# One layer of a hybrid decoder trunk: TensorE held to the program's order in the attention loop, with the value products of an earlier step placed between the score tiles

## The chip, the cores and the metric

The kernel runs on one core of a Trainium2 chip. The metric is the device time of one execution in microseconds (us); the kernel before has a median of 2955.1 us over three runs (2953.64 to 2956.42). Five engines work beside each other on that core: TensorE (PE, with its weight loads as PEld), VectorE (DVE), ScalarE (ACT), GpSimd (POOL) and SyncE (SP), which here issues most DMAs.

## The reference, cut to what matters

One layer, SEQ = 2048, D_MODEL = 1024. What the change touches is the FoX attention of eight heads of width 64 (causal, a learned decay as a bias of the logits, swept in 128-query blocks):

```python
def block(args):
    qi, ci, i = args
    s = jnp.einsum('bhqd,bhkd->bhqk', qi, kh).astype(jnp.float32) * scale
    s = s + ci[..., :, None] - c[:, :, None, :]
    qpos = i * Q_BLOCK + jnp.arange(Q_BLOCK)
    s = jnp.where(kpos[None, :] <= qpos[:, None], s, -jnp.inf)
    pr = jax.nn.softmax(s, axis=-1).astype(vh.dtype)
    return jnp.einsum('bhqk,bhkd->bhqd', pr, vh)
...
x = x + mix @ w_out[i]
x = x + jnp.square(jax.nn.relu(hm @ w_up[i])) @ w_down[i]
x = x + sigmoid(rmsnorm(x, g_ple[i]) @ w_ple_gate[i]) * (p[i] @ w_ple[i])
```

Before the attention come the input projections and an mLSTM of four heads; behind it come the output projection, the MLP and the gate.

## The kernel before, in words

The program is written with a tile framework. It is recorded engine by engine in the order of the Python code; a scheduler then chooses the order in which each engine's instructions stand, by its own estimate of when their operands are ready, and inserts semaphores. At run time each engine takes its instructions strictly in that fixed order.

The attention (the stage from 560 to 1323 us) works on pairs of heads: `for j in range(NP)` calls `fox_attn` (line 882), which goes over two heads and, within a head, over nine steps, the entries of `ROWS` (line 779). A step is one or two blocks of 128 queries whose key blocks add up to 16: query block 15 alone, then 14 and 0, 13 and 1, and so on to 8 and 6, and at last 7 alone (8 key blocks).

`fox_rows` (line 781) makes a step's probabilities. A **score tile** is a PSUM tile `s` of up to four key blocks (three buffers, `SB`): two TensorE products (lines 798 and 800, high and low part of the keys), a third for the diagonal (line 803), and one DVE instruction (line 806) that adds the `bias` tile, writes the sum to `sp` (SBUF, four buffers of eight key blocks, `SPB`) and keeps the running row maximum. Most steps have five score tiles, a head has 40. Then come `nb` (DVE, line 818), the exponentials (ACT, line 821), a 16-bit high part (ACT, line 826) and low part (POOL, sometimes DVE, line 828) in `ph` (four buffers), and a transposing DMA on SP's queue to `pt` (line 830, three buffers, eight key blocks each; two a step). A head has 17 of these units.

`fox_av` (line 834) makes the **value products** of a step: for each key block three small TensorE products (lines 846, 847, 849) from `pt`, and a copy to `og` (line 852). They run three steps late (`LAG`): `drain(LAG)` (line 856) is called at the end of each step. With three `pt` buffers, the transpose of a unit waits until the value products of the unit three before it are done.

`fill` (line 958) puts other TensorE work between score rows and value products, spread evenly over a pair's steps: for pairs 0 to 2 the projections of the next pair (`zfq`, `zv`, `zfk`, lines 260 and 271) and the embeddings (`pp`), for the last pair half of the output projection (`om`, line 641).

At the start of a head two `bias` tiles (two buffers) are loaded on SP's queue (line 890) and scaled on DVE (line 893). `bias_1` holds keys 1024 to 2047, `bias_0` keys 0 to 1023. `bias_0` of a new head takes the buffer that the last step (query block 7) of the head before it reads, so it can be loaded only after that step's DVE work, and the new head's first score tile needs it. At the end of a pair `second_keys` (lines 691 and 693) also puts the new keys of the second head in place on DVE.

Of the kernel before, what the change touches and what calls it, by code (L numbers as in the profile page):

```python
# [54 lines left out]
def hybrid_layer(ctx, tc, x, p, w_in, b_fox_f, b_mlstm_i, b_mlstm_f, w_conv, g_mix,  # L55
# [722 lines left out]

    ROWS = ((15,),) + tuple((14 - i, i) for i in range(7)) + ((7,),)

    def fox_rows(fl, fpp, h, rows, bias, fs, qkl):


        Qt, Kt, KL = qkl
        tag = f"{h}_{rows[0]}"
        nu = (sum(rows) + len(rows) + 7) // 8
        st = [fl.tile([P, 1024], F32, tag="sp", name=f"sp{tag}_{u}", bufs=SPB)
              for u in range(nu)]
        at = 0
        for r, i in enumerate(rows):  # L790
            qs = slice(i * P, (i + 1) * P)
            mx, kb, parts = None, 0, []
            while kb <= i:
                u, o = divmod(at + kb, 8)
                n = min(4, 8 - o, 8 - kb % 8, i + 1 - kb)
                ps = fpp.tile([P, 512], F32, tag="s", name=f"s{tag}_{r}_{kb}", bufs=SB)
                ks = slice(kb * P, (kb + n) * P)
                PE.matmul(ps[:, 0:n * P], lhsT=Qt[:, qs], rhs=Kt[:, ks], start=True, stop=False)  # L798
                diag = kb + n > i
                PE.matmul(ps[:, 0:n * P], lhsT=Qt[:, qs], rhs=KL[:, ks], start=False,  # L800
                          stop=not diag)
                if diag:
                    PE.matmul(ps[:, (n - 1) * P:n * P], lhsT=identb, rhs=fneg, start=False,
                              stop=True)
                m = fl.tile([P, 1], F32, tag="mx", name=f"mx{tag}_{r}_{kb}", bufs=8)
                V.tensor_tensor_reduce(out=st[u][:, o * P:(o + n) * P], in0=ps[:, 0:n * P],  # L806
                                       in1=bias[kb // 8][:, kb % 8 * P:(kb % 8 + n) * P],
                                       scale=1.0, scalar=-3.0e38 if mx is None else mx,
                                       op0=ALU.add, op1=ALU.max, accum_out=m)
                mx = m  # L810
                if parts and parts[-1][0] == u:
                    parts[-1][2] = o + n
                else:
                    parts.append([u, o, o + n])
                kb += n
            at += i + 1
            nb = fl.tile([P, 1], F32, tag="nb", name=f"nb{tag}_{r}", bufs=8)
            V.tensor_scalar(nb, mx, fs[:, 1:2], LN_P, op0=ALU.mult, op1=ALU.add)  # L818
            for u, o0, o1 in parts:
                sl_ = st[u][:, o0 * P:o1 * P]  # L820
                A.activation(sl_, sl_, AF.Exp, bias=nb, scale=fs[:, 0:1])  # L821
        pts = []
        for u in range(nu):
            ph = fl.tile([P, 2048], F16, tag="ph", name=f"ph{tag}_{u}", bufs=PHB)
            cnt[0] += 1
            A.copy(ph[:, 0:1024], st[u])  # L826
            eng = V if cnt[0] % DM == 3 else T
            eng.tensor_sub(ph[:, 1024:2048], st[u], ph[:, 0:1024])  # L828
            pt = fl.tile([P, 16, P], F16, tag="pt", name=f"pt{tag}_{u}", bufs=PTB)
            SP.dma_start_transpose(out=pt, in_=ph)  # L830
            pts.append(pt)
        return pts

    def fox_av(fl, fpp, h, rows, pts, vt, ogs):

        if not avt:
            avt.append(fpp.tile([P, 2, 2, P], F32, name="av", bufs=1))
        slot[0] ^= 1
        aps = avt[0][:, slot[0]]
        at = 0  # L840
        for r, i in enumerate(rows):
            ar = aps[:, r, 0:65]
            for kb in range(i + 1):
                pt, o = pts[(at + kb) // 8], (at + kb) % 8
                vs = vt[:, kb, (h % 2), :]
                PE.matmul(ar, lhsT=pt[:, o, :], rhs=vs[:, 0:65], start=kb == 0, stop=False)  # L846
                PE.matmul(ar[:, 1:65], lhsT=pt[:, o, :], rhs=vs[:, 65:129], start=False,
                          stop=False, skip_group_check=True)
                PE.matmul(ar, lhsT=pt[:, 8 + o, :], rhs=vs[:, 0:65], start=False, stop=kb == i)
            at += i + 1  # L850
        for r, i in enumerate(rows):
            V.tensor_copy(ogs[i // 4][:, i % 4, h % 2, :], aps[:, r, 0:65])
# [3 lines left out]
    def drain(n):  # L856
        while sum(e[0] for e in avq) > n or (avq and not avq[0][0]):
            e = avq.pop(0)
            if e[0]:
                fox_av(*e[1:])  # L860
            else:
                posts.append([PD_, *e[1:]])

# [18 lines left out]
    def fox_attn(fl, fpp, j, z, fill):  # L882
        fs, iv, vt, qkls = z
        ogs = {}
        for hh in range(2):
# [7 lines left out]
                V.tensor_scalar(b, b, fs[:, 2:3], None, op0=ALU.mult)  # L893
                bias[sg] = b
            for k, rows in enumerate(ROWS):
                pts = fox_rows(fl, fpp, h, rows, bias, fs, qkls[hh])
                for i in rows:
                    if hh == 0 and i // 4 not in ogs:
                        ogs[i // 4] = fl.tile([P, 4, 2, FD + 1], F32, tag="og",
# [3 lines left out]
                if hh == 1 and k in DONE:  # L903
                    g = DONE[k]
                    avq.append((0, fl, j, g, ogs[g], iv))
                drain(LAG)
                late()
                if h == FH - 2 and k == LK:
                    loads.append(mix_load(0, NP - 1))
# [2 lines left out]
        if j == NP - 1:  # L912
            for _ in loads[0]:
                pass
            for k in range(LAG - 1, -1, -1):
                fill(FE)
                drain(k)
                late()
            fill(1e9)
            late(all_=True)  # L920
# [36 lines left out]
    with phase("fl", 2) as fl, phase("fps", 2, PSUM) as fpp:  # L957
# [13 lines left out]
        for j in range(NP):  # L971
# [6 lines left out]
            else:  # L978
                for _ in mix_load(NP, KT):
                    pass  # L980
                fill = filler(late_parts(), FT)
            fox_attn(fl, fpp, j, box[0], fill)
            fill(1e9)
            second_keys()
            box = nxt
# [207 lines left out]
```

## Time and profile before

| what | before |
|---|---|
| median of 3 runs | 2955.1 us |
| the profiled execution's own time | 2954.44 us |
| its span, first to last instruction | 2952.7 us |
| PE busy | 2698.4 us (91%) |
| DVE busy | 1621.7 us (55%) |
| ACT busy | 1008.3 us (34%) |
| POOL busy | 698.7 us (24%) |
| mean granted TensorE clock | 0.968 of full speed |

The span is the time on the core; the execution's own time lies 1.74 us above it. The profile gives busy time by engine, the idle time before an instruction with what ended it, and for a chosen stretch the same with the granted clock and the DMA engines' busy share. PE's busy time is modelled (matmuls are pipelined), so its idle time is the safer figure.

### The profile page before, as it was taken

The numbers are of one execution on the slowest core, as the hardware profiler recorded it, in microseconds if no ns is written. First come the engines' busy times: TensorE is split into PE (matmuls) and PEld (weight loads), VectorE is DVE, ScalarE is ACT, GpSimd is POOL, SyncE is SP. The second block draws the span as 40 slices with busy tenths as digits, with TensorE's granted clock in tenths as the row PEclk, the third lists the DMA queues.
The fourth block names the chain that finished last, engine by engine and source line by source line (L and its number), as shares of the span: only waits on it lengthen the run. The fifth ranks groups of instructions, "written<-read, shape, count | busy, mean of one in ns | idle before, by whom it ended". The sixth has DMA issues, their size and how long they took to land. (4 is left out here: it accounts for less than half of the span.)

```text
span 2952.7 us, 45034 instructions
## 1 busy us (share of the span) xinstructions
PE 2698.4 (91%) x18229; PEld 1507.1 (51%) x18229; DVE 1621.7 (55%) x3633; ACT 1008.3 (34%) x1686; POOL 698.7 (24%) x435
## 2 busy tenths in 40 slices
PE   4998999888878788788999999999999999999997
PEld 2756767555454554343344444444444444444686
DVE  6464654766757657556654444444444444445636
ACT  6244444465555555553411111111111111113532
POOL 1011110244343444343122111111212111111132
PEclk9999999989899989999999999999999999999999
DMA  9212220387686879996700000000000000002623
GB/s 243 45 44 59 58 47 20 94 167 137 139 166 133 165 169 219 196 205 222 148 29 29 29 29 16 28 15 29 29 29 29 29 29 16 28 15 43 143 69 136
DMA packets 535265, 256.36 MB, mean 87 GB/s; under 512 B 432784, under 2 KB 502672, under 8 KB 535056
## 3 DMA queue, kind: packets, MB, share of 16 engines
q1 hardware_dynamic: 525296, 236.66, 35.0%
q10 hardware_dynamic: 9760, 16.82, 1.8%
q8 instruction: 142, 2.33, 0.3%
q14 instruction: 67, 0.55, 0.1%
HBM read 113.88 MB, written 32.60 MB: 50 GB/s over the span
## 5 line engine op out<-in xcount | busy, mean ns | idle before, releaser
L1054 PE MATMUL d<-wd_hl,hid 128*128 128x512 f16 x3072 | 678.2, 380 | 8.4 <-DVE x L1059 8.2
L1036 PE MATMUL h<-y1t,wu_hl 128*128 128x512 f16 x3072 | 673.5, 379 | 0.5 <-issue 0.5
L1054 PEld LDWEIGHTS <-hid 128*128 128x128 f16 x3072 | 301.3, 98 | 375.0 <-issue 15.8
L1036 PEld LDWEIGHTS <-wu_hl 128*128 128x128 f16 x3072 | 300.5, 98 | 363.2 <-ACT y1y L200 1.0
L1059 DVE SCALAR_TENSOR_TENSOR x<-d,fac,x 128x512 f32<-128x512 f32 x512 | 373.8, 747 | 132.2 <-PE d L1054 131.8
L1044 POOL TENSOR_TENSOR hid<-r,hid 128x512 f16<-128x512 f32 x128 | 174.5, 1364 | 765.2 <-ACT hid L1043 659.1
L1042 DVE SCALAR_TENSOR_TENSOR r<-h,r 128x512 f32<-128x512 f32 x128 | 88.3, 690 | 458.2 <-ACT r L1040 458.1
L1040 ACT ACTIVATE r<-h 128x512 f32<-128x512 f32 x128 | 75.9, 594 | 766.8 <-PE h L1036 763.3
L828 POOL TENSOR_TENSOR ph<-sp,ph 128x1024 f16<-128x1024 f32 x119 | 255.9, 2164 | 283.3 <-ACT ph L826 219.3
L271 PEld LDWEIGHTS <-yt 128*128 128x128 f16 x3072 | 251.6, 101 | 40.1 <-issue 13.7
L260 PE MATMUL zqk<-yt,wqk_hl 128*128 128x512 f16 x768 | 188.7, 393 | 27.9 <-DMA yt<-yy 27.9
L821 ACT ACTIVATE sp<-sp,nb,fs 128x1024 f32<-128x1024 f32 (+3 forms) x192 | 177.9, 982 | 85.2 <-DVE nb L818 60.5
L798 PE MATMUL s<-K,Q 128*128 128x512 f16 (+3 forms) x320 | 117.9, 369 | 79.4 <-DVE mx L806 76.4
L846 PE MATMUL av<-vt,pt 128*128 128x65 f16 x1088 | 121.9, 199 | 67.3 <-DMA pt<-ph 55.6
L271 PE MATMUL zvo<-wvo_hl,yt 128*128 128x256 f16 x1536 | 175.0, 275 | 4.1 <-ACT wvo_hl L155 2.8
L1007 PE MATMUL pg<-wpg_hl,y2t 128*128 128x256 f16 x1536 | 171.0, 275 | 4.7 <-DVE x L1059 4.0
L1007 PEld LDWEIGHTS <-y2t 128*128 128x128 f16 x1536 | 151.6, 99 | 24.1 <-issue 5.1
L826 ACT CAST ph<-sp 128x1024 f16<-128x1024 f32 x136 | 137.8, 1038 | 67.9 <-DMA pt<-ph 62.6
L846 PEld LDWEIGHTS <-pt 128*128 128x128 f16 x1088 | 105.3, 100 | 75.1 <-DMA pt<-ph 67.8
L806 DVE CUSTOM_DVE_ANT_0 sp<-s,bias,mx 128x512 f32<-128x512 f32 (+2 forms) x192 | 124.5, 648 | 29.4 <-POOL ph L828 14.2
L260 PEld LDWEIGHTS <-wqk_hl 128*128 128x128 f16 x768 | 77.4, 101 | 105.5 <-ACT wqk_hl L155 25.9
L641 PEld LDWEIGHTS <-mix 128*128 128x128 f16 x768 | 76.4, 102 | 101.6 <-issue 27.7
(380 smaller groups left out, 3648.2 us busy)
## 6 DMA issues: line engine op xcount, KB each, us to landing
x<-in_x_dram SPq DMA_DIRECT2D x32, 512.0 KB, 5.8
wu_st<-in_w_up_dram SPq DMA_DIRECT2D x16, 1024.0 KB
wd_st<-in_w_down_dram SPq DMA_DIRECT2D x16, 1024.0 KB, 4.9
bias<-crow SPq DMA_DIRECT2D x16, 512.0 KB, 5.9
pled<-fox_st ACTq DMA_DIRECT2D x32, 256.0 KB, 2.8
wod<-spare ACTq DMA_DIRECT2D x32, 256.0 KB, 5.0
wos<-wod SPq DMA_DIRECT2D x32, 256.0 KB, 3.9
emb<-pled SPq DMA_DIRECT2D x32, 256.0 KB, 3.0
```

What stands on the lines that cost most here:

```text
L260: PE.matmul(ps, lhsT=hl[:, a, kt, m * P:(m + 1) * P], rhs=yT[g][b][:, kt, :], start=i == 0, stop=i == 3 * KT - 1)
L271: PE.matmul(ps[:, 0:n], lhsT=yT[g][b][:, kt, o:o + P], rhs=hl[:, a, kt, 0:n], start=i == 0, stop=i == 3 * KT - 1)
L806: V.tensor_tensor_reduce(out=st[u][:, o * P:(o + n) * P], in0=ps[:, 0:n * P], in1=bias[kb // 8][:, kb % 8 * P:(kb % 8 + n) * P], scale=1.0 ...
L821: A.activation(sl_, sl_, AF.Exp, bias=nb, scale=fs[:, 0:1])
L826: A.copy(ph[:, 0:1024], st[u])
L828: eng.tensor_sub(ph[:, 1024:2048], st[u], ph[:, 0:1024])
L846: PE.matmul(ar, lhsT=pt[:, o, :], rhs=vs[:, 0:65], start=kb == 0, stop=False)
L1007: PE.matmul(ps, lhsT=aT[t // 4][ya][:, kt, o:o + P], rhs=hl[:, wa, kt, :], start=i == 0, stop=i == 3 * KT - 1)
L1036: PE.matmul(ps, lhsT=wu[:, a, kt, m * P:(m + 1) * P], rhs=y1T[g][b][:, kt, :], start=i == 0, stop=i == 3 * KT - 1)
L1044: T.tensor_sub(hid[:, 1, m], r2, hid[:, 0, m])
L1054: PE.matmul(ps, lhsT=hid[:, a, m, t * P:(t + 1) * P], rhs=wd[:, b, m, hf * 512:(hf + 1) * 512], start=i == 0, stop=i == 5)
L1059: V.scalar_tensor_tensor(xs, ps, fac, xs, ALU.mult, ALU.add)
```

## The change: what it does

Three edits go together. The attention of a pair is recorded under `manual_schedule` for PE, so that TensorE's instructions keep the order of the Python code there, while the other engines are still ordered by the scheduler. `fox_av` becomes a generator that pauses after five key blocks, then after every further five, counted over the step's 16 (`(at + kb) % 5 == 4`). And `fox_rows` is handed the generator of the step three back and takes one piece from it behind each score tile from the second on; what is left of it is done before `fill`. No instruction of TensorE is added or removed: both programs have 35645 rows on it.

```diff
-    def fox_rows(fl, fpp, h, rows, bias, fs, qkl):
+    def fox_rows(fl, fpp, h, rows, bias, fs, qkl, av):
...
-        at = 0
+        at = chunks = 0
         for r, i in enumerate(rows):
...
                 kb += n
+                chunks += 1
+                if chunks > 1:
+                    next(av, None)
...
                 PE.matmul(ar, lhsT=pt[:, 8 + o, :], rhs=vs[:, 0:65], start=False, stop=kb == i)
+                if (at + kb) % 5 == 4:
+                    yield
...
     def drain(n):
         while sum(e[0] for e in avq) > n or (avq and not avq[0][0]):
             e = avq.pop(0)
             if e[0]:
-                fox_av(*e[1:])
+                yield from fox_av(*e[1:])
...
             for k, rows in enumerate(ROWS):
-                pts = fox_rows(fl, fpp, h, rows, bias, fs, qkls[hh])
+                av = drain(LAG - 1)
+                pts = fox_rows(fl, fpp, h, rows, bias, fs, qkls[hh], av)
+                for _ in av:
+                    pass
...
                     avq.append((0, fl, j, g, ogs[g], iv))
-                drain(LAG)
                 late()
...
-                drain(k)
+                for _ in drain(k):
+                    pass
...
-            fox_attn(fl, fpp, j, box[0], fill)
+            with tc.manual_schedule(engines={mybir.EngineType.PE}):
+                fox_attn(fl, fpp, j, box[0], fill)
```

First place: TensorE in a step in the middle of head 1 (query blocks 12 and 2). `s1_12_0_8` is head 1, step 12, its first query block, key block 8; `pt1_15_0` is the first transposed unit of the step that began with query block 15; `zv1` are projections for the next pair. Only the first product of a run stands here, without weight loads and without rows that repeat. Before:

```order
L798 MATMUL s1_12_0_0_7564<-K_5163,Q0_5162 128x512
L798 MATMUL s1_12_0_4_7569<-K_5163,Q0_5162 128x512
L798 MATMUL s1_12_0_8_7574<-K_5163,Q0_5162 128x512
L798 MATMUL s1_12_0_12_7579<-K_5163,Q0_5162 128x128
L271 MATMUL zv1_14_7610<-fox_hl_5118,yt3_333 128x128
L798 MATMUL s1_12_1_0_7589<-K_5163,Q0_5162 128x384
L271 MATMUL zv1_15_7636<-fox_hl_5118,yt3_333 128x128
L846 MATMUL av_6239<-vt0_5167,pt1_15_0_7087 128x65
L846 MATMUL av_6239<-vt0_5167,pt1_15_1_7092 128x65
```

All 16 key blocks of value products stand behind the step's projections. In the changed program:

```order
L798 MATMUL s1_12_0_0_7566<-K_5163,Q0_5162 128x512
L798 MATMUL s1_12_0_4_7571<-K_5163,Q0_5162 128x512
L849 MATMUL av_6178<-vt0_5167,pt1_15_0_7134 128x65
L798 MATMUL s1_12_0_8_7591<-K_5163,Q0_5162 128x512
L849 MATMUL av_6178<-vt0_5167,pt1_15_1_7139 128x65
L798 MATMUL s1_12_0_12_7611<-K_5163,Q0_5162 128x128
L798 MATMUL s1_12_1_0_7636<-K_5163,Q0_5162 128x384
L271 MATMUL zv1_14_7661<-fox_hl_5118,yt3_333 128x128
L271 MATMUL zv1_15_7687<-fox_hl_5118,yt3_333 128x128
```

The value products now stand in pieces between the score tiles, and the projections come last and whole.

Second place: TensorE where head 1 ends and head 2, of the next pair, begins. Before:

```order
L798 MATMUL s1_7_0_4_8208<-K_5163,Q0_5162 128x512
L846 MATMUL av_6239<-vt0_5167,pt1_10_0_7869 128x65
L798 MATMUL s2_15_0_4_8370<-K_5163,Q1_5944 128x512
L846 MATMUL av_6239<-vt0_5167,pt1_10_1_7874 128x65
L798 MATMUL s2_15_0_8_8375<-K_5163,Q1_5944 128x512
L260 MATMUL zfq2_0_8525<-yt0_135,fox_hl_5118 128x512
L846 MATMUL av_6239<-vt0_5167,pt1_9_0_7993 128x65
L846 MATMUL av_6239<-vt0_5167,pt1_8_0_8117 128x65
...
L798 MATMUL s2_15_0_12_8380<-K_5163,Q1_5944 128x512
```

In the changed program:

```order
L798 MATMUL s1_7_0_4_8210<-K_5163,Q0_5162 128x512
L849 MATMUL av_6178<-vt0_5167,pt1_10_0_7921 128x65
L849 MATMUL av_6178<-vt0_5167,pt1_10_1_7926 128x65
L798 MATMUL s2_15_0_4_8375<-K_5163,Q1_5944 128x512
L849 MATMUL av_6178<-vt0_5167,pt1_9_0_8045 128x65
L798 MATMUL s2_15_0_8_8395<-K_5163,Q1_5944 128x512
L849 MATMUL av_6178<-vt0_5167,pt1_9_1_8050 128x65
L798 MATMUL s2_15_0_12_8415<-K_5163,Q1_5944 128x512
L849 MATMUL av_6178<-vt0_5167,pt1_8_0_8169 128x65
```

Before, projections and the value products of three steps stand between the third and the fourth score tile of the new head; now the fourth tile follows after two blocks of `pt1_9_1`.

Third place: SP's queue at the same boundary. Before:

```order
L830 DMA_TRANSPOSE pt1_8_1_8122<-ph1_8_1_8119 128x16x128
L830 DMA_TRANSPOSE pt1_7_0_8220<-ph1_7_0_8217 128x16x128
L716 DMA fox_st_5119<-in_w_in_dram 128x8x128
L890 DMA bias2_0_8360<-crow_382 128x1024
L945 DMA_TRANSPOSE po0_3_8296<-po0_3_8296 128x8x128
```

In the changed program:

```order
L833 DMA_TRANSPOSE pt1_8_1_8174<-ph1_8_1_8171 128x16x128
L716 DMA fox_st_5119<-in_w_in_dram 128x8x128
L895 DMA bias2_0_8365<-crow_382 128x1024
L953 DMA_TRANSPOSE po0_3_8298<-po0_3_8298 128x8x128
L833 DMA_TRANSPOSE pt1_7_0_8237<-ph1_7_0_8234 128x16x128
```

The load of `bias_0` no longer stands behind the transpose of the last step; it stands behind that of `pt1_8_1`, which waits for the value products of `pt1_9_0`.

In the last pair the `om` products move too: before, eight of them stand ahead of the value products of head 6's first step; now one or two stand behind each step.

## Rows read from the trace of the kernel before

**Rows 1.** Busy time by engine, granted clock, DMA share, GB/s: the whole attention stage.

```profile
559.90:1323.40 763.50, 609.60 (x6333) 370.39 (x6331) 490.96 (x1521) 416.05 (x531) 309.10 (x159) 0.92 0.80 163
```

**Rows 2.** PE's waits in the stage: total us, times, longest.

```profile
PE s L798 <- DVE mx L806: 76.4, 43, 4.9
PE av L846 <- DMA pt<-ph: 55.6, 35, 6.6
PE av L846 <- DVE og L852: 11.6, 6, 3.1
```

**Rows 3.** PE in order of time, one step of head 3: start, us, [idle before].

```profile
897.09 0.38 PE L260 MATMUL zfk<-yt,fox_hl 128*128 128x512 f16 x1
898.93 0.38 PE L798 MATMUL s<-K,Q 128*128 128x512 f16 x1 [1.47 <-DVE mx L806]
...
900.11 4.70 PE L260 MATMUL zfk<-yt,fox_hl 128*128 128x512 f16 x21
904.64 0.19 PE L846 MATMUL av<-vt,pt 128*128 128x65 f16 x1
...
906.12 0.38 PE L798 MATMUL s<-K,Q 128*128 128x512 f16 x1
```

**Rows 4.** Busy times in the seven head boundaries (last tile to next head's fourth): two, and sum.

```profile
733.10:753.50 20.40, 14.94 (x165) 8.67 (x162) 15.95 (x46) 5.04 (x7) 5.68 (x4) 0.92 0.96 176
...
1213.20:1238.50 25.30, 17.01 (x186) 9.31 (x185) 5.88 (x15) 10.13 (x11) 8.16 (x4) 0.87 1.09 227
sum 149.70, PE 100.64 PEld 66.47 DVE 75.87 ACT 49.36 POOL 45.37; mean PE 14.38 PEld 9.50 DVE 10.84 ACT 7.05 POOL 6.48
```

**Rows 5.** DVE in order of time at the boundary of heads 1 and 2.

```profile
733.07 0.07 DVE L806 DVE_READ_ACCUMULATOR2_ANT mx<- 128x1 f32 x1
...
750.96 0.75 DVE L893 TENSOR_SCALAR bias<-bias,fs 128x1024 f32<-128x1024 f32 x1 [1.31 <-DMA bias<-crow]
...
752.71 0.69 DVE L806 CUSTOM_DVE_ANT_0 sp<-s,bias 128x512 f32<-128x512 f32 x1
```

**Rows 6.** PE's wait at the end of that boundary.

```profile
753.47 0.39 PE L798 MATMUL s<-K,Q 128*128 128x512 f16 x1 [3.16 <-DVE mx L806]
```

**Rows 7.** SP's queue in order of time at the boundary of heads 6 and 7.

```profile
1220.50 10.31 SPq L830 DMA_TRANSPOSE pt<-ph  x3
1230.91 0.54 SPq L890 DMA_DIRECT2D bias<-crow  x1
```

**Rows 8.** The lines of the bias load and of the transposes: duration ns min/median/max; landing.

```profile
L890 SPq DMA_DIRECT2D bias<-crow x16: 332/639/1447, 540.8 to 1230.9; - x16
...
DMA to landing us min/median/max: 5.4/5.9/6.6
...
L830 SPq DMA_TRANSPOSE pt<-ph x136: 1317/2472/7229, 584.4 to 1313.0; - x136
...
DMA to landing us min/median/max: 4.3/5.2/10.1
```

**Rows 9.** DVE's groups in the stage: line, operation, count, busy us, mean ns, idle before.

```profile
L806 DVE CUSTOM_DVE_ANT_0 sp<-s,bias,mx 128x512 f32<-128x512 f32 (+2 forms) x192 | 124.5, 648 | 29.4 <-POOL ph L828 14.2 <-PE s L803 3.4 <-PE s L800 1.9
L806 DVE DVE_READ_ACCUMULATOR2_ANT mx<- 128x1 f32 x320 | 26.2, 82 | 0.0
L693 DVE COPY K<-K 64x512 f16<-64x512 f16 x14 | 13.2, 942 | 0.3
L691 DVE SCALAR_TENSOR_TENSOR KL<-zfk,K 64x512 f16<-64x512 f32 x14 | 9.7, 695 | 0.7 <-ACT K L690 0.3
```

**Rows 10.** Busy times in the stage's first 30 us.

```profile
559.90:590.00 30.10, 24.41 (x115) 10.48 (x113) 22.37 (x56) 16.41 (x20) 11.19 (x6) 0.95 0.20 45
```

**Rows 11.** Busy times and granted clock around PE's longest wait of the stage.

```profile
839.00:846.00 7.00, 1.98 (x44) 1.81 (x40) 1.89 (x2) 1.77 (x3) 1.56 (x1) 1.00 1.22 201
846.00:853.00 7.00, 5.43 (x75) 5.43 (x76) 0.85 (x4) 0.28 (x1) 0.00 (x0) 0.51 1.15 204
```

**Rows 12.** PE's waits in two stretches inside heads 6 and 7: total us, times, longest.

```profile
PE av L846 <- DMA pt<-ph: 8.6, 8, 2.0
...
PE av L846 <- DMA pt<-ph: 12.7, 6, 4.4
```

## The prediction

> **What bounds the kernel now.** I read the busy times of the stage first, then TensorE's waits in it, then single steps and the boundaries between heads in order of time. The change moves TensorE's work in the attention alone, a stretch of 763.5 us in which PE is busy 609.6, DVE 491.0, ACT 416.1 and POOL 309.1 [rows 1]. No engine is full: PE, the busiest, is idle for 763.5 - 609.6 = 153.9 us, and what ends its idle time is two things [rows 2]. In 43 waits of 76.4 us together a score tile waits for DVE, which has not yet read one of the three PSUM tiles. In 41 waits of 67.2 us value products wait for a transposed unit, or for the copy of the accumulator before them.
>
> One step shows the first kind [rows 3]. Three score tiles go out, the fourth waits 1.47 us for DVE, then come the projections (21 products in 4.70 us) and only then the value products, whose 16 key blocks take from 904.64 to 906.12, 1.48 us. So 1.48 us of work that doesn't need the score tiles stands behind the wait, in every step.
>
> The second place where PE stands still is between heads. Seven times DVE has no score tile to read until the new `bias_0` is there. These windows last 149.7 us together, with PE busy for 100.6 and so idle for 49.1 [rows 4]. PE is that busy there because the scheduler put projections and the value products of three steps between the new head's third and fourth tile. At the boundary of heads 1 and 2 the last tile of one head ends on DVE at 733.14, the scaling of `bias_0` starts at 750.96, and the first tile of the next head follows at 752.71 [rows 5]; PE's own wait at its end is 3.16 us [rows 6].
>
> **The change, part by part.** No instruction is added, so only waits can change.
>
> *Score tiles inside heads.* Of the 76.4 us of waits for DVE about 18 lie in the boundaries (six waits like that of [rows 6]), which leaves some 58 us in 37 waits, 1.6 us each. In the new order five key blocks, 5 / 16 x 1.48 = 0.46 us, stand ahead of each of the third, fourth and fifth tile: up to 1.4 us of each wait is filled. The waits are uneven (the longest is 4.9), many shorter than 1.4 and some much longer, so I take 1.15 us off each: -43 us. DVE can follow: a score tile costs it 0.65 + 0.08 = 0.73 us [rows 9], while PE's pair of score products and one piece take 0.43 + 0.46. Bounds: -58, if every wait goes; -15, if DVE is late by more than the pieces fill, since its order is still the scheduler's and weight preparation and norms stand between the tiles.
>
> *Boundaries.* Here holding the order costs. The fourth tile of the new head now follows the third after one piece, and everything behind it, projections too, waits with it. What it waits for is a chain: value products of `pt_9_0` done, `pt_8_1` issued on SP (2.5 us, the median), `bias_0` issued and landed (5.9), scaled (0.75), the first tile read (0.73) [rows 8, 5, 9]: 9.9 us, with 0.2 of PE's work beside it. That is four boundaries inside a pair at 9.7 us, 39 us. Between pairs DVE also has up to four pairs of key copies (0.70 + 0.94 each) [rows 9], a norm and a weight reduction ahead of `bias_0`; from the 19.6 us of [rows 5] I take off the transpose that no longer stands ahead of the load, and the waits for copies of value products, and come to about 15 from the last tile to the first. PE reaches its fourth tile some 2 us after that last tile, so it stands still for about 13 us, and 11 where a projection is left: 38 for three. Together 77 against 49: +28. The load itself gets earlier: before, it stood behind three transposes issued in 10.3 us [rows 7]. Bounds: +0 (7 us each), +60 (15.6 each).
>
> *Start of the stage.* In the first three steps there are no value products yet. Before, projections fill them, with 24.4 us busy in the first 30 [rows 10]; in the new order 14 score tiles and two projections, some 17 us of work, stand there. +7 us; bounds 0 and +13.
>
> *Waits for transposed units inside heads.* Value products come a fill (4 to 5 us) earlier against their step's scores, but the `pt` buffers they free come free as much earlier, so a steady step gains and loses alike: a transpose lands 5.2 us after its issue [rows 8], and is wanted a step later. In the last pair the new order helps. There 14 waits cost 21.3 us [rows 12], since eight `om` products had been used up at its start; they are now spread over the steps. I take half: -10. Bounds: -38 (about all such waits in heads), and +25, where SP's queue, with a transpose of 2.5 us twice a step and other loads between, becomes late.
>
> *Clock.* TensorE's granted clock is 0.92 in the stage [rows 1], that is 16% of the time, some 122 us, at 1.2 GHz. It fell after PE had stood still: in the 7 us behind the longest wait (6.6 us [rows 2]) it is 0.51 [rows 11]. Fewer waits inside heads, longer ones between them: -8 us, with bounds -30 and +10. The Trainium skill ("TensorE: Matmul & The Clock Gate", HAM oscillation) says that matmul bursts separated by waits start each time at the low clock, which speaks against the new order: seven longer stops, each followed by slow products. The trace agrees with it at [rows 11], where 5.4 busy us at half clock cost 2.7; by the rule alone, counting only the seven stops, the term would be +19 instead of -8.
>
> Sum: -43 + 28 + 7 - 10 - 8 = -26 us. The profiled execution took 2954.4 us (span 2952.7), 0.7 below the median of the runs shown: 2928 against it, **2929 us** against the median. What lies ahead of the stage keeps its order; behind it nothing but the starting time changes.
>
> **The rivals.** *The likeliest, as above* (0.45): 2929, own range 2908 to 2948.
>
> *More is gained* (0.18). Every stall inside a head feeds the next through three rings of buffers (`sp`, `ph`, `pt`); with value products earlier, units come free before they are wanted. Then score waits go (-58), waits for units inside heads halve (-19), the clock gives 20, boundaries and start cost what I took (+35): -62, 2893. For it: long stretches of rows where a transposed unit is waiting for its reader, not the reverse (41 waits on 136 units). Against it: DVE at 64% of the stage comes in bursts.
>
> *Slower: the boundary* (0.22). If PE stands still for s us at each of seven boundaries, the sum is 7 s - 49 - 43 + 7 - 10 - 8 = 7 s - 103: it turns at s = 14.7. The price of a boundary rests on one SP queue and one DVE order, neither of which is held. If `pt_8_1` comes late (its issue took up to 7.2 us [rows 8]) and key copies stand ahead of `bias_0`, s is 18, and the time is 2955 + 23 = 2978. For it: before, DVE's gaps are 20 to 25 us [rows 4] and PE was kept busy in them by the reordering that is now forbidden. Against it: part of each gap was the wait for transposes and value products that are now earlier.
>
> *No change* (0.15). The scheduler had already filled what there is, and a wait covered in one place comes back at the next, because the step is set by the chain from score tile through DVE, ACT, POOL and the DMA and not by PE's order; or score waits shrink by about 15 and the boundary takes them: within 6 us of 2955. For it: PE is idle only 20% of the stage.
>
> **How the numbers follow.** A measurement of this kernel can tell about 0.2%, 6 us, from no change. Faster by more: 0.45 + 0.18 = 0.63; within: 0.15; slower: 0.22. The bounds of the terms don't all fall on one side together, so the range reaches to the two rivals and a little past the first: 2885 to 2976, which leaves out less than a tenth at each end.
>
> **What would show it.** Right: PE's waits for DVE in the stage fall from 76 us to below 50, boundaries included, with none over 2 us inside heads; each boundary shows one wait of PE of 9 to 13 us ahead of a new head's fourth tile, ended by DVE; DVE's gap from the last tile to the next head's first falls from 19.6 to about 15; the stage, from first score product to last value product, takes about 737 us. The forecast is wrong if the boundary waits exceed 15 us, if waits for `pt` grow by more than 25 us, or if DVE's order, chosen anew, leaves score waits above 1.4 us in most steps.

## The result, and the profile after

| what | before | after |
|---|---|---|
| median | 2954.6 us (4 runs) | 3025.5 us (4 runs, 3020.9 to 3035.8) |
| ratio, 95% interval | | 1.025, 1.0231 to 1.0269 |
| profiled execution's own time | 2954.4 us | 3022.5 us |
| attention, first score product to last value product | 763.5 us [rows 1] | 830.4 us |
| PE idle in it | 153.9 us | 212.2 us |
| DVE busy | 1621.7 us | 1625.7 us |

The changed kernel is 2.5% slower; 66.9 of the 68.1 us by which the profiled executions differ lie in the attention. Its row answers to [rows 1]:

```profile
558.80:1389.20 830.40, 618.16 (x6326) 381.42 (x6325) 492.92 (x1530) 416.25 (x531) 312.15 (x159) 0.85 0.73 151
```

The engines do the same work in a longer time. PE's busy time rose by 8.6 us at a granted clock of 0.85 (0.92 before), its idle time by 58.3. PE's waits in that stretch (total us, times, longest), against [rows 2]:

```profile
PE s L798 <- DVE mx L806: 155.1, 43, 15.8
PE av L849 <- DMA pt<-ph: 25.2, 16, 6.1
PE av L849 <- DVE og L857: 14.0, 9, 4.2
PE pp L609 <- DVE vt L763: 11.5, 3, 6.1
```

Waits for transposed units halved (55.6 to 25.2); waits of a score tile for DVE doubled. They are of two kinds. **At the seven head boundaries** one wait each, 69.1 us together. The busy times in the stretches from a head's last tile to the next head's fourth follow: the counterparts of the two in [rows 4], and the sum of all seven.

```profile
748.20:762.45 14.25, 1.69 (x32) 1.21 (x32) 13.47 (x35) 3.50 (x4) 4.88 (x4) 0.67 0.77 178
...
1268.80:1286.30 17.50, 6.60 (x59) 3.73 (x56) 4.32 (x7) 4.98 (x6) 6.29 (x3) 0.68 1.11 230
sum 105.62, PE 23.46 PEld 14.52 DVE 56.70 ACT 24.41 POOL 25.65; mean PE 3.35 PEld 2.07 DVE 8.10 ACT 3.49 POOL 3.66
```

The stretches are shorter than before (149.7 us), but PE is idle in 105.6 - 23.5 = 82.2 us of them, against 49.1.

**Inside heads**, that is in all other score waits, they grew too, from 58.3 us to 86.2 (gaps below 0.15 us counted, which the listing leaves out). A stop ahead of a step's fifth score tile shows how. DVE in order of time, then PE:

```profile
683.76 0.69 DVE L806 CUSTOM_DVE_ANT_0 sp<-s,bias 128x512 f32<-128x512 f32 x1 [1.12 <-PE s L800]
684.37 0.08 DVE L806 DVE_READ_ACCUMULATOR2_ANT mx<- 128x1 f32 x1
687.39 0.42 DVE L582 TENSOR_REDUCE pm<-plsp 128x1 f32<-128x256 f32 x1 [2.93 <-DMA plsp<-in_p_dram]
687.72 0.74 DVE L806 CUSTOM_DVE_ANT_0 sp<-s,bias,mx 128x512 f32<-128x512 f32 x1
```

```profile
685.05 0.27 PE L798 MATMUL s<-K,Q 128*128 128x256 f16 x1
...
688.53 0.37 PE L798 MATMUL s<-K,Q 128*128 128x256 f16 x1 [3.04 <-DVE mx L806]
...
689.01 2.23 PE L271 MATMUL zv<-fox_hl,yt 128*128 128x128 f16 x19
```

DVE has read the first tile and waits 2.93 us for an embedding's load (`pm`), while three finished tiles fill the three buffers. PE stands ahead of the fifth for 3.04 us, though the projections behind it (`zv`) need nothing of all this. I laid DVE's instructions beside each wait of PE inside heads. Of the 86.2 us DVE read score tiles in 21.9, did other work in 34.5 and stood waiting in 29.8; before, 58.3 us were 21.3, 22.0 and 14.9. So the whole growth of 27.9 us stands beside DVE's other work and DVE's other waits. DVE's own waits in the stage show the reverse side:

```profile
DVE sp L806 <- PE s L800: 70.2, 29, 6.5
DVE bias L898 <- DMA bias<-crow: 46.4, 9, 8.4
DVE fss L939 <- POOL psq L937: 31.6, 9, 7.7
...
DVE pm L582 <- DMA plsp<-in_p_dram: 19.5, 7, 4.5
```

Before, DVE waited 4.6 us for score tiles and 72.8 for value products. Now it waits 70.2 for score tiles: while PE works through a step's projections in one piece, DVE has nothing to read; when the tiles come, it is often at other work, and PE waits. In the trace of before, projections (those for the embeddings and the output counted too) stand at 191 places between two score products, in that of after at 59.

### The profile page after: what moved, and what is told of

Same layout as the page of the kernel before. It is cut to its first block, busy times and chain, and to the rows that moved or that the text cites. A ratio compares the mean times of both kernels' runs of the same rounds, so it can differ in the third digit from the quotient of the medians.

```text
span 3020.8 us, 45085 instructions
## 1 busy us (share of the span) xinstructions
PE 2703.5 (89%) x18229; PEld 1517.1 (50%) x18229; DVE 1625.7 (54%) x3633; ACT 1008.1 (33%) x1686; POOL 701.5 (23%) x435
## 5 line engine op out<-in xcount | busy, mean ns | idle before, releaser
L1063 PE MATMUL d<-wd_hl,hid 128*128 128x512 f16 x3072 | 675.8, 379 | 11.8 <-DVE x L1068 11.5
L849 PE MATMUL av<-vt,pt 128*128 128x65 f16 x1088 | 137.2, 202 | 40.0 <-DMA pt<-ph 25.2
L829 ACT CAST ph<-sp 128x1024 f16<-128x1024 f32 x136 | 136.6, 1037 | 17.8 <-DMA pt<-ph 17.4
L806 DVE CUSTOM_DVE_ANT_0 sp<-s,bias,mx 128x512 f32<-128x512 f32 (+2 forms) x192 | 124.5, 649 | 24.6 <-POOL ph L831 10.0
L850 PE MATMUL av<-vt,pt 128*128 128x64 f16 x1088 | 137.0, 203 | 0.0
L852 PE MATMUL av<-vt,pt 128*128 128x65 f16 x1088 | 136.2, 201 | 0.0
```

The source lines that it names most:

```text
L1063: PE.matmul(ps, lhsT=hid[:, a, m, t * P:(t + 1) * P], rhs=wd[:, b, m, hf * 512:(hf + 1) * 512], start=i == 0, stop=i == 5)
```

## The experiments

Theory: held to a fixed order, PE can't go around a stop of DVE; the loss is DVE's other work ahead of score tiles inside heads, and the chain through `bias_0` at the boundaries. Rivals, numbered in the expectations: the value products between the tiles themselves; the order chosen for DVE; the fixed order as such; the boundaries alone. The medians of the kernel before, run again beside each group of these runs, lay between 2950.7 and 2954.7 us; ratios are against it, with 95% intervals. "Boundary waits" are PE's waits ahead of a new head's fourth score tile, "inside heads" are all its other waits of score tiles for DVE.

### The two halves of the change

```diff
# e1: from the changed kernel
-            with tc.manual_schedule(engines={mybir.EngineType.PE}):
-                fox_attn(fl, fpp, j, box[0], fill)
+            fox_attn(fl, fpp, j, box[0], fill)
# e2: to the kernel before
+            with tc.manual_schedule(engines={mybir.EngineType.PE}):
+                fox_attn(fl, fpp, j, box[0], fill)
```

> The new placement of the value products, but TensorE ordered by the scheduler again. My theory (the loss is the fixed order: TensorE can no longer put projections between score tiles while DVE works on something else): 2945 to 2965 us; TensorE's waits of score tiles for DVE in the attention back from 155 to 70 to 95 us, the seven boundary waits back from 69 to about 20. Rival 1 (the value products between the score tiles are themselves what slows the step): 3000 to 3030, score waits above 130.

Measured: 2966.0 us, ratio 1.0049 (1.0033 to 1.0065).

> TensorE held to the program's order, but the value products at the end of the step as before the change. My theory: the fixed order costs the more the less stands between the score tiles, so this is slower than the changed kernel: 3040 to 3100 us, score waits 180 to 250 us. Rival 1 (the interleaving costs, not the order): 2955 to 2990. Rival 2 (interleaving makes no difference at all): 3015 to 3035.

Measured: 3057.7 us, 1.0361 (1.0343 to 1.0378). PE's waits, e1 (two rows), then e2:

```profile
PE s L798 <- DVE mx L806: 69.1, 52, 5.4
PE av L849 <- DMA pt<-ph: 67.4, 50, 4.1
```

```profile
PE s L798 <- DVE mx L806: 193.4, 83, 18.2
```

The fixed order alone costs 3.6%; the new placement takes 32 us of that back. In e2's trace the waits inside heads are 122.3 us and those at the boundaries 71.8, against 58.3 and 19.5 in the kernel before; with the pieces between the tiles, in the changed kernel, they are 86.2 and 69.1. So the pieces fill 36 us of waits inside heads, and the fixed order had first added 64. With the order free, the placement costs 0.5%, just above the expected span, and it shows as waits for units (55.6 to 67.4), not for DVE. Rival 1 falls: the hold is what costs.

### What stops TensorE inside heads

e5 takes much of DVE's other work out of the attention: maxima and scales become constants, the norm goes, and differences go to POOL, so that its output is no longer that of the layer. The core of the edit, called lean below:

```diff
-        pw, sc = pow2_scale(mp, npart, name)
+        if leanf[0]:
+            pw, sc = one[:, 0:1], one[:, 3:4] if name.startswith("wo") else one[:, 1:2]
...
-        V.tensor_sub(hl[:, 1], sf, hl[:, 0])
+        (T if leanf[0] else V).tensor_sub(hl[:, 1], sf, hl[:, 0])
...
-            V.tensor_reduce(pm, pin, axis=AX.X, op=ALU.max, apply_absolute_value=True)
...
+            psc, pe = one[:, 2:3], pec
...
-            eng = V if cnt[0] % DM == 3 else T
+            eng = T
...
-        rr = rstd_of(ss, 8, f"frr{j}_{g}", YS)
...
-        V.tensor_mul(og, og, rr.unsqueeze(2).to_broadcast([P, 8, FD]))
```

> The changed kernel with DVE's other work in the attention taken away: the maxima and scales of weights and embeddings are constants, the norm of the heads' outputs is left out, and the differences for the low parts of ph, hl, plsp and po go to POOL. My theory (TensorE's longer stops inside heads are DVE standing on or working at other things, some 60 of the 86 us): waits of score tiles inside heads fall to 15 to 35 us, 2935 to 2965 us. Rival 3 (the fixed order alternates between TensorE waiting for DVE and DVE waiting for TensorE by itself, whatever else DVE does): waits inside heads stay above 60 us, 2995 us or more.

Measured: 2971.0 us, 1.0051 (1.0034 to 1.0067). Stage, and PE's waits:

```profile
568.74:1332.16 763.42, 588.93 (x6326) 369.11 (x6325) 336.24 (x1054) 415.93 (x531) 373.94 (x189) 0.88 0.81 165
```

```profile
PE s L801 <- DVE mx L809: 90.0, 25, 12.7
PE av L852 <- DMA pt<-ph: 67.2, 19, 8.4
```

DVE is busy 336.2 us in the stage, 157 less than in the changed kernel. Of the 90.0 us, 65.4 are the seven boundaries, so 24.6 are left inside heads, in the middle of the expected 15 to 35. The attention is 67 us shorter. The time came out 6 us above the expected span: the attention begins 10 us later, and the waits for units rose from 25 to 67. Why they rose is open: POOL now makes all differences of `ph`, but in f3 below it does so too, and there these waits are 27.2.

```diff
# e6: from the changed kernel
-            with tc.manual_schedule(engines={mybir.EngineType.PE}):
+            with tc.manual_schedule(engines={mybir.EngineType.PE, mybir.EngineType.DVE}):
```

> The changed kernel with DVE held to the program's order too, so that its other work stands between the steps and not between score tiles. My theory (the bursts are work that has to be done somewhere and waits where it stands; the place that the scheduler chose is better than the program's): 3040 to 3120 us. Rival 5 (the order that the scheduler chose for DVE is the fault): below 3000 us, with waits inside heads under 50 us.

Measured: 3156.0 us, 1.0677 (1.0657 to 1.0697): worse than expected. PE waits 266.9 us for score tiles. The program's order is worse for DVE than the scheduler's: DVE itself now stands 54.0 us ahead of differences of `ph`, until ACT is done (26.5 in the changed kernel), and 56.4 ahead of `plsp` (7.7). A third order of DVE was not tried.

```diff
# f3: from the changed kernel
+        def load(t):
...
+            SP.dma_start(out=pin, in_=p[t * P:(t + 1) * P, :])
...
-            SP.dma_start(out=pin, in_=p[t * P:(t + 1) * P, :])
...
             nxt_ = pre(t + 1) if t + 1 < t1 else None
+            if t + 2 < t1:
+                load(t + 2)
...
-            eng = V if cnt[0] % DM == 3 else T
+            eng = T
```

> The changed kernel; only two of DVE's other jobs are mended: all differences for ph go to POOL, and the embeddings' rows are loaded one token ahead, so that their maximum doesn't wait for the load. In the changed kernel these two stand in eight of the stops inside heads, 28 us together. My theory: waits inside heads fall from 86 to 60 to 72 us, 3000 to 3012 us. Rival (other work moves up into the same places, or POOL becomes late): within 10 us of 3025.

Measured: 3004.2 us, 1.0179 (1.0165 to 1.0192). The time fell as expected, but not by the waits I named: those inside heads are 84.2 us (60 to 72 expected). DVE still waits 18.2 us for the embeddings' rows, against 19.5. At the place below, SP's queue took the load behind two transposes. SP, then DVE:

```profile
629.59 6.06 SPq L840 DMA_TRANSPOSE pt<-ph  x2
635.70 0.88 SPq L580 DMA_DIRECT2D plsp<-in_p_dram  x1
```

```profile
640.04 0.42 DVE L585 TENSOR_REDUCE pm<-plsp 128x1 f32<-128x256 f32 x1 [1.41 <-DMA plsp<-in_p_dram]
```

PE's idle time fell by 14 us, 9 of them in `pp` waiting for `vt` (11.5 to 2.4), and its busy time by 8.5. So this run doesn't bear the theory out: it took the `ph` differences from DVE, and the waits inside heads stayed. Beside them DVE's other work fell from 34.5 us to 29.8, and its standing still stayed at 30.0.

### The boundaries

```diff
# e4: from the changed kernel
-            for sg in (1, 0):
+            for sg in (1, 0) if h == 0 else ():
```

> The changed kernel, but only head 0 loads its two bias tiles and every head uses them: the loads, the scalings and the wait of a new head for bias_0 are left out. My theory (the boundaries are about 69 us of waits, of which the bias chain is the cause at four and a part at three; the other 86 us of the score waits lie inside heads and stay): boundary waits fall to 20 to 40 us, waits inside heads stay at 75 to 95; 2985 to 3003 us. Rival 4 (the boundaries are the whole loss): 2950 to 2960.

Measured: 3000.7 us, 1.0157 (1.0136 to 1.0177). The boundary waits fell from 69 to 15 us, below the expected 20 to 40, and waits inside heads rose from 86 to 115, above the expected 75 to 95: of 54 us half comes back. Rival 4 falls.

e3 also cuts the projections `zfq` and `zfk` into four pieces each (`z_pieces`, a pause after every two of its eight `kt`) and hands projections out behind each tile:

```diff
                 if chunks > 1:
                     next(av, None)
+                fill(n, False)
...
-                fill(sum(rows) + len(rows) + RC)
+                fill(RC)
```

> The changed kernel, but the projections, cut into pieces of 6 products, also stand between the score tiles in the program, a share behind every tile. My theory (TensorE comes to a tile too early, because DVE also works on other things; with 1.8 us of work per tile instead of 0.9 the ring of three tiles bridges stops of 2 to 4 us): waits inside heads fall from 86 to 20 to 45 us, boundaries from 69 to 55 to 65; 2950 to 2985 us. Rival 3 (DVE's order is simply bad and stops the step wherever PE's work stands): within 15 us of 3025.

Measured: 2980.6 us, 1.0097 (1.0082 to 1.0112). The time is as expected and the reason isn't. PE's waits, and the row of DVE at the longest of them:

```profile
PE s L817 <- DVE mx L825: 109.7, 31, 14.4
PE av L869 <- DMA pt<-ph: 34.9, 15, 5.5
```

```profile
784.14 0.69 DVE L825 CUSTOM_DVE_ANT_0 sp<-s,bias 128x512 f32<-128x512 f32 x1 [9.98 <-POOL ph L851]
```

The boundary waits fell to 19 us, with projections now between the new head's first tiles; the rest is 91 us, of which 14 stand ahead of a head's first two tiles (5.6 in the changed kernel), so inside the heads proper 77 are left of 81. In the longest stop DVE waits for an `sp` buffer until POOL's subtraction is done. POOL is not slow there, it is late itself: the buffers `ph` also serve the heads' outputs `po`, and ACT, which writes `ph` ahead of POOL, stands until the store of `po` is through:

```profile
779.72 1.04 ACT L849 CAST ph<-sp 128x1024 f16<-128x1024 f32 x1 [4.04 <-DMA mixd<-po]
```

So projections between tiles mend the boundaries and hardly the stops inside heads.

```diff
# e8: from e3 (and f1 from the kernel before): early bias
+    def bias_load(fl, h, sg):
+        b = fl.tile([P, 1024], F32, tag=f"bias{(h + sg) % 2}", name=f"bias{h}_{sg}", bufs=1)
...
-            for sg in (1, 0):
-                b = fl.tile([P, 1024], F32, tag="bias", name=f"bias{h}_{sg}", bufs=2)
...
+            for sg in (0, 1):
+                b = early.pop((h, sg), None)
...
             for k, rows in enumerate(ROWS):
+                if k == len(ROWS) - 1 and h + 1 < FH:
+                    early[h + 1, 0] = bias_load(fl, h + 1, 0)
```

> The split experiment's kernel (order held), but the two bias buffers change places from head to head, so that bias_0 of a new head takes the buffer of bias_1, which the last step doesn't read, and its load is asked for ahead of the last step. My theory: the wait at the four boundaries inside a pair falls from 3 to 7 us to below 2, those between pairs by 3 to 5, and as in the experiment without loads about half comes back inside heads: 2960 to 2974 us. Rival (bias_1, now late, takes its place): 2976 to 2986.

Measured: 2974.5 us, 1.0065 (1.0048 to 1.0082), just above the expected span. The 19 us ahead of the fourth tiles went; one wait of 10.8 us came ahead of a sixth tile, where DVE reads `bias_1`, now the later load. The rival named it, at one boundary of seven.

### The same mends with the order free

> The program of the split experiment (value products and pieces of projections behind every score tile), with TensorE ordered by the scheduler. My theory (what the fixed order costs is the freedom to put projections where DVE is late, and pieces in fixed places return only part of it): 2940 to 2965 us, 15 to 40 us below the split experiment's 2980.6. Rival 6 (with fine pieces the held order costs nothing, and the 30 us that the split experiment lacks come from the program itself): 2975 to 2990.

Measured: 2965.3 us, 1.0033 (1.0019 to 1.0046): 15 us below the same program held, at the edge of my span and outside the rival's.

> The kernel before the change (order free, value products at the end of a step) with the bias buffers changing places from head to head and the load of bias_0 asked for ahead of the last step. My theory: at the four boundaries inside a pair TensorE's waits for DVE (3.0, 0, 4.3 and 1.5 us in the trace of before) go, between pairs 1 to 2 us each: 2940 to 2952 us. Rival (the scheduler covers the boundary anyhow, and chooses another order): within 6 us of 2954.

Measured: 2952.8 us, 0.9998 (0.9987 to 1.0009): no difference, the rival's answer. In the scheduler's order that chain had cost little: the boundary waits were 19.5 us before and are 13.9.

```diff
# f2: from f1
-    DONE = {3: 3, 4: 0, 7: 2, 8: 1}
+    DONE = {4: 3, 5: 0, 7: 2, 8: 1}
...
-    ROWS = ((15,),) + tuple((14 - i, i) for i in range(7)) + ((7,),)
+    ROWS = ((3, 11), (15,)) + tuple((14 - i, i) for i in (0, 1, 2, 4, 5, 6)) + ((7,),)
```

> As the kernel before with early bias_0, and a head begins with query blocks 3 and 11 (three score tiles that read bias_0) in place of 15, so that bias_1, now the late one, is wanted a tile later. If the late bias_1 takes the place of bias_0: 3 to 8 us below the run without the new order of blocks. If bias_1 is no matter: equal to it within 4 us.

Measured: 2962.3 us, 1.0030 (1.0015 to 1.0045): slower, with longer waits for units (66.2 us, f1 51.7), which neither case foresaw, and shorter ones for DVE (73.4, f1 86.7).

> The kernel before with early bias_0 and the embeddings' rows loaded one token ahead. Before, DVE stood 14.2 us for those rows; where TensorE's order is free this is covered by projections. My theory: 0 to 6 us below the run with early bias_0 alone. Rival (equal cost in both orders): 10 to 14 us below it.

Measured: 2949.9 us, 0.9993 (0.9979 to 1.0006): 3 us below f1, less than can be told apart; the rival's 10 to 14 are not there.

### Both causes taken away, held and free

g1 is e8 with the edits of f3; g2 is e5 with early bias; h1 is lean on the kernel before, h2 the same with early bias.

> TensorE held to the program's order with every mend that leaves the result whole: value products and pieces of projections behind every score tile, early bias_0, all differences for ph on POOL, the embeddings' rows asked for one token ahead. The two edits of DVE's and POOL's work brought 21 us in the changed kernel. If mends add up: 2950 to 2962 us. If, with pieces between the tiles, DVE's stops are covered already (and POOL is late for sp instead): 2968 to 2980. Either way not below the kernel before by more than 6 us.

Measured: 2974.1 us, 1.0068 (1.0051 to 1.0085), equal to e8: these mends don't add up.

> The lean kernel (changed kernel, DVE's other work left out: constants for the maxima and scales of weights and embeddings, no norm of the heads' outputs) with early bias_0. In the lean kernel seven boundary waits of 7.3 to 12.7 us, 65 together, are left of 90 us of score waits, and the attention takes 763 us. My theory (two separate causes: DVE's other work inside heads, the bias chain at the boundaries): the four waits inside pairs, 32 us, fall to below 10; attention 738 to 752 us, 2946 to 2960 us in all. Rival (a freed boundary is given back as later units, the lean kernel's waits for pt growing from 67 us): attention 758 us or more, 2965 to 2975.

Measured: 2935.6 us, 0.9941 (0.9924 to 0.9957), better than expected. The boundary waits went from 65.4 us to none, but in part they only moved: 34.4 us now stand ahead of a new head's fifth to tenth tiles, most of them at the sixth, where DVE waits for `bias_1`.

> The kernel before (order free, value products at the end of a step) with DVE's other work left out as in the lean kernel. The lean edits took 55 us from the changed kernel. My theory (the free order had already covered most of DVE's stops with projections): they take only 5 to 25 us here, 2930 to 2950 us. Rival (DVE's other work costs the same in both orders): 2895 to 2910 us.

Measured: 2935.0 us, 0.9945 (0.9926 to 0.9964), as the theory had it.

> The same with early bias_0, the free counterpart of the lean held kernel with early bias_0 (2935.6 us). If the held order costs nothing by itself once DVE is free and bias_0 early: within 10 us of 2935 or above. If it costs something by itself: below 2925 us.

Measured: 2926.1 us, 0.9915 (0.9899 to 0.9932), 9.5 us below g2, so just inside the "within 10 us" of the case without such a cost. The attention of g2, of h1 and of h2:

```profile
567.84:1296.05 728.21, 588.56 (x6326) 368.29 (x6325) 339.55 (x1054) 417.11 (x531) 373.52 (x189) 0.90 0.84 173
```

```profile
571.35:1299.54 728.19, 596.06 (x6326) 366.94 (x6325) 345.87 (x1054) 416.85 (x531) 373.76 (x189) 0.92 0.84 170
```

```profile
569.24:1287.01 717.77, 590.09 (x6326) 361.11 (x6325) 345.47 (x1053) 416.27 (x531) 373.71 (x189) 0.93 0.86 173
```

The pairs split the loss, the changed kernel (held, pieces between the tiles) against the kernel before (free) in each: 3025.5 - 2954.6 = 70.9 us with all of DVE's work; 2971.0 - 2935.0 = 36.0 in the lean form; 2935.6 - 2926.1 = 9.5 with early bias as well. In the attention: 66.9, 35.2, 10.4. So some 35 us of the loss go with DVE's other work (the lean edit takes 54.5 us from the changed kernel and 19.6 from the one before) and some 26 with the bias chain, in this order of removal. The kernels of a pair did not all run beside each other: by their ratios to the kernel before (2.5, 1.1 and 0.3%) the shares are 42 and 24, by the attention's lengths 32 and 25. Lean also loads POOL more (312 to 374 us in the attention), so that the 35 are the whole edit's. The last 10 us don't show a cost of the held order in itself: PE's waits at a new head's first ten score tiles, where `bias_1` is now the late one, are 37.2 us in g2 and 25.4 in h2, and those for units 62.6 and 30.5. What makes up these 10 us stays open.

### A version below both

The low part's differences go from DVE to POOL: in h4 those of `ph`, in h3 also those of the weights and of `po`; order free, early bias, loads as in f4.

```diff
# h3
-        V.tensor_sub(hl[:, 1], sf, hl[:, 0])
+        low[0].tensor_sub(hl[:, 1], sf, hl[:, 0])
...
-        V.tensor_sub(mq[:, 1], og, mq[:, 0])
+        T.tensor_sub(mq[:, 1], og, mq[:, 0])
```

> Order free as before the change, early bias_0, embeddings' rows asked for one token ahead, and the differences for ph, for the weights' low part and for po moved from DVE to POOL: what of the lean edits leaves the result whole. Leaving out all of DVE's other work took 25 us from the free kernel with early bias_0. If DVE's bursts are what counts: 2930 to 2944 us. If POOL, with longer subtractions now ahead of the units, becomes late: 2950 or more.

> The same with only the differences for ph moved to POOL (17 in the attention, 25 us of DVE's time before). Same rule: 2938 to 2948 us if DVE's bursts count, 2950 or more if POOL becomes late.

Measured: h3 2975.3 us, 1.0079 (1.0066 to 1.0092); h4 2955.5, 1.0010 (1.0001 to 1.0019). POOL became late: DVE waits 69.7 us for `sp` until POOL is done in h3 and 64.7 in h4, against 41.7 in f4, from which both start. No kernel with the whole result came below the kernel before by more than 0.1%.

## Why the prediction was wrong, point by point

PE's idle time and busy time in the attention, by the terms of the sum:

| term | predicted | measured |
|---|---|---|
| score tiles inside heads | -43 (58 to 15) | +28 (58.3 to 86.2) |
| boundaries, PE idle | +28 (49 to 77) | +33 (49.1 to 82.2) |
| start, units inside heads, all else idle | +7 - 10 = -3 | -3 (46.5 to 43.8) |
| clock (busy time) | -8 | +9 (609.6 to 618.2) |
| sum | -26 | +67 |

**The step that failed is "Score tiles inside heads"**, 71 us of the 93 between forecast and result, and in it the sentence "DVE can follow: a score tile costs it 0.65 + 0.08 = 0.73 us, while PE's pair of score products and one piece take 0.43 + 0.46". It compared PE with DVE reading tiles; DVE's other work entered only the bound of -15. DVE's tile work in the stage is 124.5 + 81.6 + 26.5 = 232.6 us of 492.9:

```profile
L806 DVE CUSTOM_DVE_ANT_0 sp<-s,bias,mx 128x512 f32<-128x512 f32 (+2 forms) x192 | 124.5, 649 | 24.6 <-POOL ph L831 10.0 <-DVE mx L806 2.2 <-PE s L803 1.2
L806 DVE CUSTOM_DVE_ANT_0 sp<-s,bias 128x512 f32<-128x512 f32 (+3 forms) x128 | 81.6, 637 | 91.0 <-PE s L800 69.7 <-POOL ph L831 20.3 <-DVE bias L898 0.3
L806 DVE DVE_READ_ACCUMULATOR2_ANT mx<- 128x1 f32 x320 | 26.5, 83 | 0.0
```

The other 260 us, and DVE's waits in them, stand in the same queue; up to 1.4 us of value products can't cover stops of 2 to 6.5 us, and 21 waits inside heads are longer than 2. And the term's bounds, -58 to -15, left no room for longer waits, though the fixed order takes away what had kept DVE's stops from PE: the projections at 191 places. I counted that loss at the boundaries and not inside the heads. The filling itself was priced well: against the same fixed order without the pieces (e2) the waits inside heads are 36 us shorter, where the sum had 43. What failed is the 58 us that it was taken from, the waits of the free order; the fixed order alone makes them 122.3. e5 bears out that DVE's other work is what PE meets there: with 157 of its 260 us gone, 24.6 us of waits are left.

**Boundaries**: 69.1 us of waits against 77 predicted. The sum set these 77 against 49 of whole idle time and left out the idle time beside the waits, 13.1 us, so its +28 came near the +33 partly by luck, through two errors that offset each other. The four inside pairs took 6.1 to 8.3 us (9.7 predicted), those between pairs 11.9, 11.7 and 15.8 (13, or 11 with a projection left; 13, 13 and 11 make 37, not 38). The chain is the one described; in the first, DVE in order of time:

```profile
655.89 0.35 DVE L857 COPY og<-av 128x65 f32<-128x65 f32 x2
664.06 0.75 DVE L898 TENSOR_SCALAR bias<-bias,fs 128x1024 f32<-128x1024 f32 x1 [7.81 <-DMA bias<-crow]
664.73 0.41 DVE L582 TENSOR_REDUCE pm<-plsp 128x1 f32<-128x256 f32 x1
665.05 0.68 DVE L806 CUSTOM_DVE_ANT_0 sp<-s,bias 128x512 f32<-128x512 f32 x1
```

**Start and units** were right together. In the first 30 us PE is busy 17.8 us (24.4 in [rows 10]), the 7 predicted; part of it is booked above, since score waits for DVE in these 30 us grew from 2.7 to 7.1. That units would come free earlier was right: outside the boundaries their waits fell from 31.5 to 19.7 us, 12 where the term had 10. The rest of the fall from 55.6 to 25.2 lies at the boundaries (24.2 to 5.5). Waits of `pp` for `vt` (1.3 to 11.5) took most of the gain inside heads.

**Clock**: the wrong sign. Behind three boundary waits (8.0, 11.9 and 15.8 us) the granted clock of the next 7 us:

```profile
665.80:672.80 7.00, 7.00 (x85) 6.45 (x85) 3.01 (x14) 3.97 (x4) 0.53 (x1) 0.63 0.55 78
762.45:769.45 7.00, 7.00 (x85) 4.63 (x86) 5.91 (x21) 4.06 (x4) 0.09 (x1) 0.71 0.67 140
1184.46:1191.46 7.00, 7.00 (x37) 3.40 (x38) 2.90 (x10) 2.37 (x2) 2.88 (x1) 0.62 1.05 276
```

So each is followed by a stretch partly at the lower level, 1.2 GHz, as [rows 11] had shown. The rule of the Trainium skill weighed in the prediction ("TensorE: Matmul & The Clock Gate", HAM oscillation) had the sign right (+19 by it, +9 measured).

**Of the signs named ahead**, boundary waits of 9 to 13 us ended by DVE came in two of seven, and DVE's gap at the boundary of heads 1 and 2 fell to 13.5 us, near the 15; score waits below 50 us and a stage of 737 did not come. Of the signs against, one boundary wait of seven exceeded 15 us, and waits for `pt` fell. Score waits above 1.4 us did not come in most steps: 23 waits inside heads are longer, in 72 steps, against 18 before; what grew is those over 2 us, from 9 to 21. The rival that forecast a slower kernel had the sign, with PE standing still for 18 us at each boundary and a turn at 14.7. It stands 82.2 / 7 = 11.7 us, so that mechanism alone would not have made the kernel slower.

## What to carry to other kernels

Before an engine's order is fixed by hand, read what the free order does in the waits of its partner: an engine that looks idle 20% may be covering another's stops with work from elsewhere. Take what a placement fills from the waits under the fixed order, not from those of the free one. When asking whether a reader can follow, count all that stands in its queue, with the waits, not the reading alone.

## What the hardware did that I had not expected

DVE's key copies, short operations from SBUF to SBUF, took up to nearly eight times as long where they met an instruction of POOL. Two copies of keys of one shape at the boundary of heads 1 and 2, then the POOL instruction beside the first:

```profile
752.24 1.62 DVE L693 COPY K<-K 64x512 f16<-64x512 f16 x1
...
755.59 0.29 DVE L693 COPY K<-K 64x512 f16<-64x512 f16 x1
```

```profile
751.59 2.12 POOL L831 TENSOR_TENSOR ph<-sp,ph 128x1024 f16<-128x1024 f32 x1 [0.22 <-ACT ph L829]
```

Of the 28 such copies (lines 693 and 773) in the changed kernel's attention, the 17 at 0.29 us have no POOL instruction beside them for more than 7% of their time; the other 11 take 0.41 to 2.25 us and lie beside one for 64 to 93%, and each of the 11 ends 0.15 us after that instruction, however long it took. The score tiles' instruction, which also reads PSUM, shows no such spread: in its form without `mx` none of 128 takes more than 0.69 us. The Trainium skill ("Trainium Architecture — The Big Picture", What this means for kernel authors) says that DVE and GpSimd share a pair of SBUF ports under an exclusive lock; the trace agrees with a copy that waits until POOL is done: the long one above ends at 753.86, POOL's instruction at 753.71. I had priced these copies at their mean, 0.94 us.
